# Where the paged decode's value pages are multiplied: pairs inside the seams behind the output projections and in cross attention, in place of dummy products

## The chip, the cores and the metric

The kernel runs on one core of a Trainium2 chip. The metric is the device time of one launch in microseconds, the median of several runs. TensorE (PE) multiplies and transposes, and loads its weights ahead (PEld); VectorE (DVE) and ScalarE (ACT) work elementwise and along rows; GpSimd (POOL) here does small power functions and issues the gathers of cache pages; SyncE (SP) issues the other loads and stores. The order of each engine's instructions is fixed when the program is recorded.

## What is computed

One layer of a hybrid decoder on two groups that share weights: a prompt of 1024 rows by 1024, and eight sample rows, each of which attends to 64 cached pages of 128 positions.

```python
q, k, v, logf, u, z = mixer_inputs(rmsnorm(xp, g_mix[l]), w_in[l], b_f[l], g_sgu_v[l])
xp = xp + merge_heads(fox_prompt(q, k, v, logf), sgu_prompt(u, z, w_s[l], b_s[l]),
                      g_att_out[l], g_sgu_out[l], w_o[l])
mk, mv = memory_kv(mem_prompt, g_mem[l], w_ck[l], w_cv[l])
xp = xp + cross_attend(rmsnorm(xp, g_cross[l]), mk, mv, w_cq[l], w_co[l])
f, conv_p = conv_ffn(rmsnorm(xp, g_ffn[l]), jnp.zeros((bp, CONV_W - 1, 2 * D_FF), xp.dtype),
                     w_up[l], conv_w[l], conv_b[l], w_down[l])
xp = xp + f
...
att = fox_sample(q, k, v, logf, cache_k[l], cache_v[l], cache_logf[l], page_table)
```

`fox_sample` is what the text calls the decode: scores of one query row against all cached keys of its sequence, a softmax with a forget gate, and the weighted sum of the cached values. In the kernel the cache of a sequence is read in sixteen steps, each of which gathers 128 pieces of four positions: one tile of 128 x 2048 numbers, which the text calls a page (128 K pages and 128 V pages in all, 1 MB each).

## The kernel before

**Stages.** The prompt goes in two halves of 512 rows (four row blocks of 128). After the input projection and attention each half hf runs through three stages: the output projection w_o with its residual ("mid"), cross attention with its own projections w_cq and w_co, and the convolutional FFN. Every large product is made of three (high and low halves of both operands: L272 to L274, L280 to L284, L1063 to L1065 and L1081 to L1083), so PE does most of the work.

**A seam.** Between an output projection and the next stage the rows must be normalized and transposed, which nothing of the next stage can precede. `out_proj` (L1023) does the left 512 columns for all row blocks, then the right 512 columns in groups: row block 0, row block 1, row blocks 2 and 3 together. After each group `residual` (L1011) adds the product to x on DVE (L1015) and squares it on ACT (L230, `ssq_into`). `factor` (L1028) makes 1/rms of a row block from that: ACT L1031, then POOL L1032 (a power). Behind w_co, `scaled` and `both` scale the rows: y0, y1 on ACT, y2 on ACT (L1044) and y3 on DVE (L1045), the last two in halves. Behind w_o the rows go on unscaled. `norm_T` (L1104) transposes two row blocks at a time on PE (L1124, t0 = 0, then t0 = 2), and `split` makes the high half on ACT (L238) and the low half on DVE (L239). `first` starts the next stage's product with what is there: `gemm3_late` (L276) first issues the products that need high halves (L280 and L281: one column half each), and then those with the low half (L284). The seams in the trace: mid0 at about 545 to 580 us, w_co to the first FFN at about 690 to 708, mid1 at 1170 to 1185, w_co to the second FFN at 1320 to 1336.

**Dummies.** For the late half of the seams behind w_co (`late`), `fill` (L1098) issues eight products (L1102, 128 x 256) of numbers that are at hand into a psum tile which the transposes then overwrite. Nothing reads them.

**The decode in the background.** `sample()` is a generator. The prompt's generator yields the time that it thinks its last piece takes, and the loop at the end of the program runs a decode step whenever enough has gathered (`PACE`, by stage), but none while `held[0]` is set. A K step gathers a K page with POOL (L1428), multiplies it by the query on DVE (L1444) and sums it (L1448). A V step gathers with POOL (L1489) and multiplies on PE (L1495) into one psum tile for a sequence. V steps come in pairs of pages: a pair is requested in one step of the decode and multiplied in the next. The trace shows a pair as sixteen L1495, the order as eight. K and V pages share one pool of four buffers (`NKV`), so a page's gather waits until the page four before it has been used. `held[0]` is set after the group of row blocks 2 and 3 and cleared when `norm_T` ends. `mix` runs two generators side by side; `gating(1)`, a piece of the second half's spatial gating, runs beside the first half's cross attention (ratio 0.05), and what is left of it then runs later.

**Order.** The tile framework records the instructions through a scheduler: `tc.high_priority()` raises a piece, and `tc.issue_after(x)` keeps an instruction behind x. The order on each engine is what comes out of that.

## Time and profile before

| | us |
|---|---|
| runs: 1789.9, 1795.0, 1800.49; median | 1795.0 |
| the profiled execution, its span | 1791.7 |
| PE busy in it | 1735.9 |
| DVE busy | 1399.9 |
| ACT busy | 733.5 |
| POOL busy | 488.3 |
| the 1024 products of V pages (L1495), busy | 127.1 |
| gathers of V pages on POOL (L1489, 128) | 160.8 |

The span holds the whole execution. A row of the timeline names the start, the duration, the engine, the line and operation, what is written from what, and how many such instructions follow one another; in brackets stands the idle time before it, and what ended it. PE's ends are modelled and rows overlap, so the time that an instruction occupies PE is read from the distance of two starts. Tiles: `u` is the pool of working rows and their split halves, `ba` and `bb` are two psum pools, `fac` holds 1/rms, `gp` the gains, `wh` and `wl` a weight's halves, `kv` a page, `dv` the sum of values, `s` the decode's scores.

### The profile page before, as it was taken

To read this page: it belongs to the slowest core of one execution; us is meant where nothing else is said; L and a number is where in the kernel's file an instruction comes from. 1 tells how busy PE (TensorE), PEld (TensorE's weight loads), DVE (VectorE), ACT (ScalarE), POOL (GpSimd) and SP (SyncE) were. 2 spreads that over 40 slices of the span, in tenths; PEclk is the share of its full clock that TensorE was granted. 3 is DMA by queue.
4 is the path that set the end of the run, shared out by engine and by line. 5 is a ranking of instruction groups with operands and counts; after the bars stand their busy time and mean duration, and the time that the engine had idled before them with its cause. 6 is when DMAs were issued, how large, how long until landed. Compare 5 with 4: busy or idle time off the path is not lost.

```text
span 1791.7 us, 25124 instructions
## 1 busy us (share of the span) xinstructions
PE 1735.9 (97%) x9653; PEld 1285.7 (72%) x9653; DVE 1399.9 (78%) x1733; ACT 733.5 (41%) x1374; POOL 488.3 (27%) x461
## 2 busy tenths in 40 slices
PE   8999999889999999999999999999999999999997
PEld 5787777655677666767777777766666778768875
DVE  4689658989788986989999999898885549855344
ACT  6332355566643635333333244335353233333232
POOL 1252234443222332333322223433322112102110
PEclk9999999999999999999999999999999999999999
DMA  8786798777697975779788788988879587568982
GB/s 291 297 304 226 294 334 319 259 264 244 254 403 279 363 299 224 282 285 345 290 301 313 291 317 311 376 306 346 320 280 350 214 306 249 191 260 297 359 310 80
DMA packets 157074, 521.06 MB, mean 291 GB/s; under 512 B 20874, under 2 KB 40842, under 8 KB 124186
## 3 DMA queue, kind: packets, MB, share of 16 engines
q0 software_dynamic: 57168, 341.14, 50.0%
q1 hardware_dynamic: 92874, 165.73, 26.5%
q10 hardware_dynamic: 6912, 12.59, 1.9%
q8 instruction: 76, 1.25, 0.3%
q14 instruction: 44, 0.36, 0.1%
HBM read 495.47 MB, written 23.93 MB: 290 GB/s over the span
## 4 chain that ended last, share of the span: by engine, by line
PE 53%; issue 9%; DMA 8%; DVE 6%; ACT 2%; POOL 2%; POOLq 0%; DVEq 0%; ACTq 0%; SPq 0%
DMA kv<-cache_v,io 6%; PE ba L272 6%; PE ba L274 6%; PE ba L273 6%; PE dv L1495 4%; PE bb L272 3%; PE bb L273 3%; PE bb L274 3%; PE ba L1063 1%; DVE s L1448 1%; PE ba L1064 1%; PE ba L1065 1%; PE dv L331 1%; DMA kv<-cache_k,io 1%; PE dv L1774 1%
## 5 line engine op out<-in xcount | busy, mean ns | idle before, releaser
L235 ACT ACTIVATE wh<-wr 128x1024 fp32r<-128x1024 f32 (+2 forms) x220 | 228.6, 1044 | 443.3 <-PE ba L273 142.3
L236 DVE TENSOR_TENSOR wl<-wr,wh 128x1024 fp32r<-128x1024 f32 (+2 forms) x220 | 262.7, 1200 | 165.1 <-PE ba L274 57.4
L1428 POOL DMA_INDIRECT kv<-cache_k,io x128 | 186.9, 1460 | 606.8 <-DVE s L1448 327.2
L1444 DVE TENSOR_TENSOR kv<-kv,d 128x1024 f32<-128x1024 f32 (+1 forms) x156 | 258.0, 1681 | 32.6 <-DMA kv<-cache_k,io 32.6
L1448 DVE TENSOR_REDUCE s<-kv 128x16 f32<-128x1024 f32 (+1 forms) x156 | 258.4, 1672 | 0.0
L1489 POOL DMA_INDIRECT kv<-cache_v,io x128 | 160.8, 1256 | 239.4 <-PE dv L1495 155.2
L272 PE MATMUL ba<-u,wh 128*128 128x512 f32 x528 | 209.3, 397 | 0.0
L274 PE MATMUL ba<-u,wl 128*128 128x512 f32 x528 | 209.0, 396 | 0.0
L273 PE MATMUL ba<-u,wh 128*128 128x512 f32 x528 | 208.5, 395 | 0.5 <-DVE u L239 0.5
L272 PE MATMUL ba<-wh,u 128*128 128x512 f32 (+1 forms) x495 | 186.1, 379 | 0.9 <-ACT u L235 0.9
L273 PE MATMUL ba<-wl,u 128*128 128x512 f32 (+1 forms) x495 | 185.1, 375 | 1.3 <-DVE wl L236 1.3
L274 PE MATMUL ba<-wh,u 128*128 128x512 f32 (+1 forms) x495 | 183.4, 375 | 0.0
L1495 PE MATMUL dv<-kv,s 128*32 128x512 f32 x1024 | 127.1, 598 | 1.6 <-DMA kv<-cache_v,io 1.6
L274 PEld LDWEIGHTS ba<-u,wl 128*128 128x128 f32 x528 | 99.2, 188 | 29.0 <-issue 6.5
L272 PEld LDWEIGHTS ba<-u,wh 128*128 128x128 f32 x528 | 99.3, 188 | 26.4 <-issue 4.8
L273 PEld LDWEIGHTS ba<-u,wh 128*128 128x128 f32 x528 | 99.2, 188 | 25.2 <-issue 2.3
L272 PEld LDWEIGHTS ba<-wh,u 128*128 128x128 f32 x495 | 93.0, 188 | 25.0 <-issue 6.5
L272 PE MATMUL bb<-u,wh 128*128 128x512 f32 x272 | 108.7, 400 | 0.0
L274 PE MATMUL bb<-u,wl 128*128 128x512 f32 x272 | 108.0, 398 | 0.0
L273 PE MATMUL bb<-u,wh 128*128 128x512 f32 x272 | 107.9, 397 | 0.0
L273 PEld LDWEIGHTS ba<-wl,u 128*128 128x128 f32 x495 | 93.0, 188 | 20.1 <-DVE wl L236 1.9
L274 PEld LDWEIGHTS ba<-wh,u 128*128 128x128 f32 x495 | 92.9, 188 | 19.5 <-issue 1.6
(454 smaller groups left out, 3310.6 us busy)
## 6 DMA issues: line engine op xcount, KB each, us to landing
wr<-w_up SPq DMA_DIRECT2D x88, 512.0 KB
kv<-w_up POOLq DMA_DIRECT2D x22, 1024.0 KB
wr<-w_down SPq DMA_DIRECT2D x40, 512.0 KB
kv<-w_down POOLq DMA_DIRECT2D x11, 1024.0 KB
wr<-w_in SPq DMA_DIRECT2D x16, 512.0 KB
wr<-w_o SPq DMA_DIRECT2D x16, 512.0 KB
wr<-w_cq SPq DMA_DIRECT2D x16, 512.0 KB
wr<-w_co SPq DMA_DIRECT2D x16, 512.0 KB
```

The costliest lines, as they stand in the source:

```text
L235: nc.scalar.activation(h, src, AF.Copy)
L236: nc.vector.tensor_tensor(l, src, h.bitcast(F32), op=ALU.subtract)
L272: mmul(out, sh, mh, start=(i == 0), stop=False)
L273: mmul(out, sh, ml, start=False, stop=False)
L274: mmul(out, sl, mh, start=False, stop=(i == n - 1))
L331: mmul(ps[32 * j : 32 * j + 32, :w], xT[:, k, :] if nk == 8 else xT[:, k * 8 : k * 8 + 32], raw[:, q, j * w : (j + 1) * w], start=(k == 0) ...
L1063: mmul(pss[i], mh[k][:, tb], wh, start=(k == korder[0]), stop=False)
L1428: nc.gpsimd.indirect_dma_start(kv, None, a["cache_k"], off(kidx[:, b, ch : ch + 1]))
L1444: nc.vector.tensor_tensor(kvv[:, i : i + m, :], kvv[:, i : i + m, :], qb.unsqueeze(1).broadcast_to((P, m, 512)), op=ALU.mult)
L1448: nc.vector.tensor_reduce(s[:, ch * 4 + i : ch * 4 + i + m, :].rearrange("p k h -> p (k h)"), kvv[:, i : i + m, :].rearrange("p k (h d) -> ...
L1489: nc.gpsimd.indirect_dma_start(kv, None, a["cache_v"], off(kidx[:, b, ch : ch + 1]))
L1495: mmul(dv[32 * j : 32 * j + 32, :], s[:, ch * 4 : ch * 4 + 4, :].rearrange("p k h -> p (k h)"), kvv[:, j, :], start=(ch == 1), stop=(ch == ...
```

## The change

1. `out_proj` sets `held[0]` before the products of row blocks 2 and 3 at the right columns instead of behind them, and there calls `ask_ahead`, which requests V pages for up to two pairs.
2. `norm_T` calls `give_now(2)`, which multiplies up to two pairs that have been requested: in front of the late transposes in place of `fill` (`fill` remains where no pair is at hand), and in every `norm_T` in front of `first` of the second half.
3. Cross attention multiplies up to one pair at the start of each `gather`; between `keys(2)` and the output projection (`lazy[0]`) pairs are multiplied nowhere else.
4. The decode keeps its pairs in a queue (`pend`), counts those requested (`asked`) and those whose softmax exists (`able`), and ends a sequence (`vend`) when its last pair is done and none is pending. In "mid" stages it requests a pair only while more than two can be requested, or more than two are due.
5. In `both` y2's scaling is issued behind the newest square (row block 3's).
6. `gating(1)` runs beside cross attention at ratio 0.08 instead of 0.05.

```diff
+            squared[:] = [newest(ENG.Activation)]
...
-        def both(r2, r3):
+        def both(r2, r3, end):
 
             y2, y3 = U([P, D]), U([P, D])
             for c in (slice(0, 512), slice(512, D)):
-                nc.scalar.activation(y2[:, c], xt[2][:, c], AF.Copy, scale=r2)
+                with tc.issue_after(end):
+                    nc.scalar.activation(y2[:, c], xt[2][:, c], AF.Copy, scale=r2)
...
             for group in ((0,), (1,), (2, 3)):
+                if len(group) == 2:
+                    held[0] = True
+                    if burst:
+                        burst[0]()
...
-                held[0] = len(group) == 2
                 yield 5.2
...
-                ys.append(partial(both, factor(2), factor(3)))
+                end = squared[0]
+                ys.append(partial(both, factor(2), factor(3), end))
...
-                if late and kk == 0:
+                if late and kk == 0 and not (burst and burst[1](2)):
                     fill(tr, hs)
...
+            if t0 and burst:
+                burst[1](2)
             first(hs, ls, c)
...
         def gather(h):
+            if burst:
+                burst[1](1)
...
+        lazy[0] = True
         keys(2)
...
             gather(h)
             yield 4
+        lazy[0] = False
...
+        pend, masked = [], []
+        asked, able = [0], [0]
+        def ask():
+
+            vb, i = divmod(asked[0], 8)
+            if i == 0:
+                dv[vb] = DV()
+            two = [(2 * i, KV()), (2 * i + 1, KV())]
+            if i % 2:
+                two.reverse()
+            pend.append((vb, i, [vstep(vb, c, st[vb], dv[vb], kv) for c, kv in two]))
+            asked[0] += 1
+
+        def give():
+
+            vb, i, mms = pend.pop(0)
+            mms[1]()
+            mms[0](newest(ENG.PE))
+            if i == 7:
+                vm[vb] = vmask(vb, dv[vb])
+                masked.append(vb)
+
+        def ask_ahead():
+            while len(pend) < 2 and asked[0] < able[0] and (not pend or asked[0] % 8):
+                ask()
+
+        def give_now(n):
+            k = 0
+            while pend and k < n:
+                with tc.issue_after(newest(ENG.PE)):
+                    give()
+                k += 1
+            return k
+
+        burst[:] = [ask_ahead, give_now]
...
+            if masked and not pend:
+                vend(masked[0], vm[masked.pop()])
...
+                able[0] = b * 8
...
+            while pend and not lazy[0]:
+                give()
+            n = (g - 16 - VLAG) // 2
+            due = min(n + (g - 16 - VLAG) % 2, 64) - asked[0]
+            spare = able[0] - asked[0] if phase[0][:3] == "mid" and g < 128 else 9
+            if not pend and due > 0 and (spare > 2 or due > 2):
+                ask()
...
-                ys = yield from mix(cross(xt, sq), gating(1), 0.05)
+                ys = yield from mix(cross(xt, sq), gating(1), 0.08)
```

The order on the engines at three places. In the changed program L1124 is L1131, L1495 is L1509, L1044 is L1047 and L1031 is L1033; L230, L238, L280, L281 and L284 keep their numbers.

PE in the seam from w_co to the first FFN, before, from the first late transpose on (`u_6373` is y2; `bb_6340` and the like are psum tiles for transposes, `ba_6304` is the FFN's first product):

```order
L1124 MATMUL bb_6405<-cp,u_6373 128x128
L280 MATMUL ba_6304<-u_6338,wh_6301 128x256
L281 MATMUL ba_6304<-u_6338,wl_6300 128x256
L284 MATMUL ba_6304<-u_6306,wh_6301 128x256 x2
L284 MATMUL ba_6304<-u_6317,wh_6301 128x256 x2
L284 MATMUL ba_6304<-u_6328,wh_6301 128x256 x2
L284 MATMUL ba_6304<-u_6339,wh_6301 128x256 x2
L1102 MATMUL ba_6379<-u_6305 128x256
L1124 MATMUL ba_6396<-cp,u_6373 128x128
L1124 MATMUL ba_6414<-cp,u_6373 128x128
L1102 MATMUL ba_6379<-u_6305 128x256
L1102 MATMUL ba_6379<-u_6316 128x256 x2
```

and now (`u_6360` is y2, `u_6361` y3; `kv` and `dv` belong to the decode):

```order
L1131 MATMUL ba_6409<-cp,u_6360 128x128
L280 MATMUL ba_6291<-u_6325,wh_6288 128x256
L281 MATMUL ba_6291<-u_6325,wl_6287 128x256
L284 MATMUL ba_6291<-u_6293,wh_6288 128x256 x2
L284 MATMUL ba_6291<-u_6304,wh_6288 128x256 x2
L284 MATMUL ba_6291<-u_6315,wh_6288 128x256 x2
L284 MATMUL ba_6291<-u_6326,wh_6288 128x256 x2
L1509 MATMUL dv_5415<-kv_6177,s_2862 32x512 x4
L1509 MATMUL dv_5415<-kv_6178,s_2862 32x512 x4
L1509 MATMUL dv_5415<-kv_6215,s_2862 32x512
L1131 MATMUL ba_6366<-cp,u_6361 128x128
L1131 MATMUL ba_6391<-cp,u_6361 128x128
```

In place of the dummies stand a whole pair and one row of a second; four transposes of y2 (the first row is the last of them) stand ahead of the last L280, one before. Behind the twelve transposes, of which two are shown, follow the other seven rows of the second pair.

PE in the seam from w_co to the second FFN, before (`u_11104` is y2, `u_11105` y3):

```order
L284 MATMUL ba_11035<-u_11037,wh_11032 128x256 x2
L284 MATMUL ba_11035<-u_11048,wh_11032 128x256 x2
L284 MATMUL ba_11035<-u_11059,wh_11032 128x256 x2
L284 MATMUL ba_11035<-u_11070,wh_11032 128x256
L1124 MATMUL ba_11127<-cp,u_11104 128x128
L284 MATMUL ba_11035<-u_11070,wh_11032 128x256
L1102 MATMUL bb_11110<-u_11036 128x256 x2
L1102 MATMUL bb_11110<-u_11047 128x256 x2
L1102 MATMUL bb_11110<-u_11058 128x256 x2
L1102 MATMUL bb_11110<-u_11069 128x256 x2
L1124 MATMUL bb_11110<-cp,u_11104 128x128
```

and now (`u_11081` is y2, `u_11082` y3):

```order
L1131 MATMUL bb_11132<-cp,u_11082 128x128
L280 MATMUL ba_11012<-u_11046,wh_11009 128x256
L281 MATMUL ba_11012<-u_11046,wl_11008 128x256
L284 MATMUL ba_11012<-u_11014,wh_11009 128x256 x2
L284 MATMUL ba_11012<-u_11025,wh_11009 128x256 x2
L1131 MATMUL ba_11123<-cp,u_11081 128x128
L1131 MATMUL ba_11123<-cp,u_11082 128x128
L1131 MATMUL ba_11123<-cp,u_11081 128x128
L1131 MATMUL ba_11123<-cp,u_11082 128x128
L284 MATMUL ba_11012<-u_11036,wh_11009 128x256 x2
L284 MATMUL ba_11012<-u_11047,wh_11009 128x256 x2
L1509 MATMUL dv_10153<-kv_10932,s_8605 32x512 x4
```

The first row here is the last of twelve transposes of y2 and y3 in a row; before, all late transposes but one stood behind the products. Two pairs stand behind the last L284, one row of which is shown.

ACT in the seam from w_co to the first FFN, before (`sqx` holds the sums of squares, `u_4762` is row block 2, `u_4764` row block 3):

```order
L230 ACTIVATE junk_6274,sqx_5897<-u_4762 128x512
L238 ACTIVATE u_6338<-bb_6340,gp 128x256
L1031 ACTIVATE fac_1257_6279<-sqx_5897,part_5898 128x1
L1044 ACTIVATE u_6373<-u_4762,fac_1257_6279 128x512 x2
L230 ACTIVATE junk_6277,sqx_5897<-u_4764 128x512
L238 ACTIVATE u_6338<-bb_6340,gp 128x256
L1031 ACTIVATE fac_1258_6282<-sqx_5897,part_5898 128x1
L230 ACTIVATE junk_6285,ssu_5123<-u_5806 128x512
```

and now:

```order
L230 ACTIVATE junk_6274,sqx_5930<-u_4762 128x512
L238 ACTIVATE u_6325<-bb_6327,gp 128x256
L1033 ACTIVATE fac_1259_6279<-sqx_5930,part_5931 128x1
L230 ACTIVATE junk_6277,sqx_5930<-u_4764 128x512
L1047 ACTIVATE u_6360<-u_4762,fac_1259_6279 128x512 x2
L1033 ACTIVATE fac_1260_6282<-sqx_5930,part_5931 128x1
L238 ACTIVATE u_6325<-bb_6327,gp 128x256
L238 ACTIVATE u_6303<-ba_6391,gp 128x256
```

Row block 3's square has moved ahead of y2's scaling, and the squares of the gating (`ssu`) have left this place.

More of the change, by code (lines that the diff above doesn't have):

```diff
@@ L1006, in build @@
     held = [False]
+    squared = []
     def squares():
@@ L1366, in build @@
     last = {}
+    burst, lazy = [], [False]
     bgs, acc, phase = [], [0.0], ["p1", None]
@@ L1524, in decode @@
         st, A, dt_, pm, dg, dv, vm = ([None] * 8 for _ in range(7))
-        pend = []
+        pend, masked = [], []
[27 more added lines that the diff above has]
+        burst[:] = [ask_ahead, give_now]
         st[0] = prep(0)
@@ L1528, in decode @@
             b, ch = divmod(g, 16)
-            if ch == VLAG + 1 and 2 <= b < 10:
-                vend(b - 2, vm[b - 2])
+            if masked and not pend:
+                vend(masked[0], vm[masked.pop()])
             if ch == 0 and 1 <= b < 9:
@@ L1545, in decode @@
                     pm[b] = soft_max(b, st[b], dt_[b])
-            if pend:
-                pend.pop()()
-                pend.pop()(newest(ENG.PE))
-                if vch == 15:
-                    vm[vb] = vmask(vb, dv[vb])
-            vb, vch = divmod(g - 16 - VLAG, 16)
-            if 0 <= vb < 8 and vch % 2:
-                if vch == 1:
-                    dv[vb] = DV()
-                two = [(vch - 1, KV()), (vch, KV())]
-                if vch % 4 == 3:
-                    two.reverse()
-                pend += [vstep(vb, c, st[vb], dv[vb], kv) for c, kv in two]
+            while pend and not lazy[0]:
[5 more added lines that the diff above has]
+                ask()
             yield left
+        if masked:
+            vend(masked[0], vm[masked[0]])
+        burst.clear()
     rows8 = []
```

## The prediction

> **What bounds the kernel now.** I read the head of the page first, then busy time in stretches of 100 us, then finer stretches, then the timelines of the seams.
>
> ```profile
> span 1791.7 us, 25124 instructions
> PE 1735.9 (97%) x9653; PEld 1285.7 (72%) x9653; DVE 1399.9 (78%) x1733; ACT 733.5 (41%) x1374; POOL 488.3 (27%) x461
> ...
> 600.00:700.00 100.00, 94.63 (x459) 65.49 (x456) 83.60 (x100) 49.28 (x111) 32.63 (x27) 1.00 0.79 308
> ...
> 800.00:900.00 100.00, 100.00 (x478) 73.11 (x477) 97.00 (x89) 31.89 (x51) 31.80 (x24) 1.00 0.85 323
> 1300.00:1400.00 100.00, 97.22 (x534) 66.30 (x533) 65.54 (x94) 43.65 (x85) 26.09 (x27) 1.00 0.83 315
> ```
>
> Columns after the length: PE, PEld, DVE, ACT and POOL busy, granted clock, DMA share, GB/s. PE is the bound: a microsecond is won only where PE idles or multiplies something nobody needs. In 800 to 900 DVE, at 97.00, is nearly a second bound. The change touches the two seams where w_co ends and the FFN begins; I call them B (near 700 us) and D (near 1330 us). In finer stretches:
>
> ```profile
> 680.00:685.00 5.00, 5.00 (x30) 2.74 (x30) 5.00 (x5) 3.16 (x3) 0.99 (x2) 1.00 0.00 0
> ...
> 695.00:700.00 5.00, 2.15 (x12) 1.76 (x13) 1.99 (x6) 4.29 (x12) 1.11 (x2) 0.96 1.00 419
> 700.00:705.00 5.00, 5.00 (x31) 4.75 (x29) 3.05 (x9) 1.63 (x7) 1.01 (x1) 0.70 0.68 270
> ```
>
> In 680 to 685 the DMA queues have nothing to do; in 695 to 700 they are full. There PE first stands still for 2.85 of 5 us; then it is busy, but at a granted clock of 0.70, which costs 5 x 0.30 = 1.5 us. PE's timeline of B:
>
> ```profile
> 694.00 0.39 PE L280 MATMUL ba<-u,wh 128*128 128x256 f32 x1 [0.32 <-ACT u L238]
> ...
> 695.51 0.38 PE L280 MATMUL ba<-u,wh 128*128 128x256 f32 x1 [0.57 <-DVE u L239]
> ...
> 697.71 0.33 PE L1124 MATMUL bb<-cp,u 128*128 128x128 f32 x1 [1.70 <-ACT u L1044]
> 698.68 0.39 PE L280 MATMUL ba<-u,wh 128*128 128x256 f32 x1 [0.64 <-ACT u L238]
> ...
> 699.02 1.46 PE L284 MATMUL ba<-u,wh 128*128 128x256 f32 x8
> 700.27 0.41 PE L1102 MATMUL ba<-u 128*128 128x256 f32 x1
> ...
> 700.77 1.84 PE L1102 MATMUL ba<-u 128*128 128x256 f32 x7
> 702.41 1.21 PE L1124 MATMUL ba<-cp,u 128*128 128x128 f32 x7
> ...
> 704.07 0.38 PE L280 MATMUL ba<-u,wh 128*128 128x256 f32 x1
> ```
>
> Brackets hold the idle time and what ended it: 0.32 + 0.57 + 1.70 + 0.64 = 3.23 us of waiting, and 0.41 + 1.84 = 2.25 us of dummies (L1102). The longest wait is for y2, scaled on ACT. The chain behind it, on ACT, POOL and DVE:
>
> ```profile
> 695.35 0.29 ACT L1031 ACTIVATE fac<-sqx,part 128x1 f32<-128x1 f32 x1
> 696.32 1.33 ACT L1044 ACTIVATE u<-u,fac 128x512 f32<-128x512 f32 x2 [0.68 <-POOL fac L1032]
> 697.56 0.61 ACT L230 ACTIVATE junk<-u 128x512 bf16<-128x512 f32 x1
> ...
> 698.53 0.28 ACT L1031 ACTIVATE fac<-sqx,part 128x1 f32<-128x1 f32 x1
> ...
> 694.05 0.68 DVE L1015 TENSOR_TENSOR u<-ba,u 128x512 f32<-128x512 f32 x1
> ...
> 699.47 0.88 DVE L1045 TENSOR_SCALAR u<-u,fac 128x512 f32<-128x512 f32 x2 [0.33 <-POOL fac L1032]
> ```
>
> Row block 3 is complete on DVE by 694.73, but its Square runs on ACT only at 697.56, behind y2. ACT itself waits 0.68 us for POOL just before y2. D, with the pair that stands before it:
>
> ```profile
> 1322.23 1.92 PE L1495 MATMUL dv<-kv,s 128*32 128x512 f32 x16
> 1324.08 0.50 PE L1083 MATMUL ba<-wh,u 128*128 128x512 f32 x1
> ...
> 1325.11 0.27 PE L1468 MATMUL ms<-cp,pm 128*8 128x128 f32 x1
> 1326.43 0.39 PE L280 MATMUL ba<-u,wh 128*128 128x256 f32 x1 [1.05 <-DVE u L239]
> ...
> 1329.34 0.51 PE L284 MATMUL ba<-u,wh 128*128 128x256 f32 x2 [0.18 <-DVE u L239]
> 1330.61 0.33 PE L1124 MATMUL ba<-cp,u 128*128 128x128 f32 x1 [0.77 <-ACT u L1044]
> ...
> 1330.90 1.11 PE L1102 MATMUL bb<-u 128*128 128x256 f32 x8
> ...
> 1333.02 0.17 PE L1616 MATMUL ms<-cp,mT 8*8 8x8 f32 x1 [0.51 <-DVE s L1483]
> 1333.42 0.33 PE L1124 MATMUL bb<-cp,u 128*128 128x128 f32 x1 [0.23 <-DVE u L1045]
> ...
> 1335.13 0.36 PE L280 MATMUL ba<-u,wh 128*128 128x256 f32 x1
> ...
> 1326.32 0.96 ACT L238 ACTIVATE u<-ba,gp 128x256 fp32r<-128x256 f32 x2
> ```
>
> Here 2.74 us are waits and 1.11 us dummies. So B and D hold 3.23 + 2.25 + 2.74 + 1.11 = 9.33 us that useful work could fill, and the low clock another 1.5. The first two rows give the price of a pair: 1324.08 - 1322.23 = 1.85 us of PE. Its products are needed anyway: moving a pair gains only what it covers at its new place.
>
> **Seam B.** In the new order two pairs, 3.70 us, stand in it, and the dummies are gone: 9 of their 16 rows behind the eight L284, then twelve late transposes, then 7 rows, then the first late L280. Before y2, ACT now does row block 3's Square, which fits mostly into its 0.68 us of waiting; y2 keeps its time to about 0.1 us. fac3 loses the Square from its path, so y3, ready at 699.47 + 0.88 = 700.35 before, comes about 0.6 us earlier. Four transposes of y2 instead of one stand ahead of the last L280, all waiting for the same y2, so the 1.70 us stays. I count from the end of the eight L284, 700.27: 9/16 of 3.70 is 2.08; thirteen transposes lie between 702.41 and 704.07, 0.128 each, twelve 1.53; 7/16 of 3.70 is 1.62. The late L280 then comes at 700.27 + 2.08 + 1.53 + 1.62 = 705.5, against 704.07: the seam is 1.4 us longer and holds 3.70 us that stood elsewhere, a gain of 2.3. y3 is there before the transposes reach it, so the pairs hide it; without them it would be waited for. New on POOL are the pairs' V pages ahead of fac0 and fac1, the last of them behind a buffer that a K page's reduce on DVE sets free. That reduce stands on DVE ahead of the residual that fac1 needs anyway, so fac1 loses one issue of about a microsecond at most, and y1, which follows it, is wanted only after w_co's last 48 products. The pages are asked for before those products, 48 x 0.26 = 12 us ahead (four of them lie between 1324.08 and 1325.11 in D's rows below), where the DMA queues stood empty. Bounds: everything filled, 3.23 + 2.25 = 5.5 of gain; nothing, if a page lands late. For the clock I take half of 1.5, 0.7 of gain, bounds 0 and 1.5.
>
> **Seam D.** Two pairs stand behind the last L284, but twelve late transposes, y3's among them, now stand ahead of the last L280 and of all L284, and on ACT seven splits (L238) stand ahead of y2. From the end of w_co the path is, by the rows of B: Square 0.61 and fac 0.29, each twice, and y2 1.33, with seven splits at the 0.48 of D's ACT row: 1.80 + 1.33 + 3.36 = 6.5 us, against 1330.61 - 1325.11 = 5.5 before. Then PE does sixteen transposes, 2.05, L280 and eight L284, 1.3 by the 1.11 of eight products as wide, and the pairs last: 6.5 + 3.4 + 3.7 = 13.6 us, of which 3.7 are pairs; 9.9 without them, against 1335.13 - 1325.11 = 10.0. The end of w_co comes earlier by the pair that no longer stands there, which is not counted twice. I take 0, bounds 2 of gain (DVE's K work is gone sooner) and 2 of loss (a split waits longer).
>
> **Cross attention and w_o.**
>
> ```profile
> 618.35 3.72 PE L1188 MATMUL ba<-t,u 128*128 128x256 f32 x16 [1.23 <-ACT t L1175]
> ...
> 626.71 1.92 PE L1495 MATMUL dv<-kv,s 128*32 128x512 f32 x16 [0.33 <-DMA kv<-cache_v,io]
> ...
> 1259.55 1.13 PE L1216 MATMUL ba<-u,t 128*128 128x512 f32 x2 [1.03 <-ACT u L1209]
> ...
> 1179.52 0.39 PE L280 MATMUL bb<-u,wh 128*128 128x256 f32 x1 [1.70 <-ACT u L238]
> ```
>
> A pair now stands before each gather (L1216) and would cover the third row's 1.03; the first row's wait is in front of L1188, where none is put. I take 1.0 of gain, bounds 2.3 (both waits) and 2 of loss (a late page like the second row's, 0.33, several times). Between w_o and the cross projections the 1.70 us of the last row stays: the pair stood behind it and does so still, so 0, give or take 1.
>
> **Elsewhere.** Pages and pairs are the same in number. The sample's end comes 4 us earlier in PE's order, and PE still has the prompt's last products after it, so the tail gains nothing. Gating at 0.08 moves its products from the FFN into cross attention, the same work: 0, give or take 1. K pages cost DVE:
>
> ```profile
> L1444 DVE TENSOR_TENSOR kv<-kv,d 128x1024 f32<-128x1024 f32 (+1 forms) x156 | 258.0, 1681 | 32.6 <-DMA kv<-cache_k,io 32.6
> L1448 DVE TENSOR_REDUCE s<-kv 128x16 f32<-128x1024 f32 (+1 forms) x156 | 258.4, 1672 | 0.0
> ```
>
> (258.0 + 258.4) / 128 pages = 4.0 us each. By the order, 62 instead of 63 are done when the first FFN begins: 4.0 us more for DVE there, against 100 - 97.00 = 3.0 spare in one of its three stretches of 100; 0, up to 1 of loss.
>
> **Sum.** -2.3 - 0.7 + 0 - 1.0 = -4.0 us: 1791.7 - 4.0 = 1787.7 for a profiled execution. The median of the runs, 1795.0, lies 3.3 above the profiled span, which is the whole of that execution; on the runs' scale 1791.0.
>
> **Rivals.** Half a percent of 1795.0 is 9 us, about what a measurement of this kernel can tell from no change.
>
> (a) The seams close wholly. For it: waits and dummies together are as long as four pairs, 9.33 against 7.4 us. Against it: in both seams y2's wait stands in PE's order ahead of the pairs, and PE takes them in order. It gives -9.33 - 1.5 - 2.3 = -13.1: 1778.6, 1782 on the runs' scale.
>
> (b) The clock falls without the dummies, and pairs run at half rate. For it: 0.70 in 700 to 705 although no wait in B passed 1.70 us. Against it: 0.96 in the stretch before. Pairs in B would cost 3.7 more, -4.0 + 0.7 + 3.7 = +0.4: 1792.1, 1795. The Trainium skill, "TensorE: Matmul & The Clock Gate", Part 1, states a gate that is either full or half, set by how busy the array was in a free-running window of about 3.4 us; by that rule the dummies bought nothing in B, as the 0.70 among them agrees, and pairs behind the same stall would start slow too.
>
> (c) Slower: K pages pushed into the first FFN. While a seam is held no page is started, and V pages fill the four kv buffers; four K pages then stand in a row on POOL behind fac3, and the count is one behind. If DVE has to take these five at once, 5 x 4.0 = 20.0 us meet 3.0 of spare, wl (L236) comes late and PE waits 17.0; with 4.0 won, +13.0: 1804.7, 1808. It decides once more than 4.0 + 3.0 = 7.0 us of DVE work, two pages, must be done at once. For it: DVE at 97.00. Against it: the count of one page.
>
> (d) The pairs only change places: the seams grow by what they take in, 1791.7, 1795.
>
> **Chances.** Forecast 0.46, (a) 0.18, (b) 0.07, (c) 0.20, (d) 0.09. The forecast's own bounds, its terms not all at their ends together, are 1784 to 1797; the range, out past (a) and to the near side of (c), is 1778 to 1806. Faster by over 0.5% (under 1786): (a) and a third of the forecast, 0.33. Slower (over 1804): (c) and 0.03 of the others' upper ends, 0.23. Within: 0.44.
>
> **What would show it.** B right: no L1102, two pairs between the last L284 and the late L280, Square of row block 3 before y2, the wait for y2 still there at 1.5 to 2 us, and 4 us or more of new cover. D right: a wait of 3 to 4 us in front of the twelve transposes. Clock: 700 to 705 above 0.85. (a): waits under 1 us in both. (c): PE under 99 us in 700:800 or 800:900, waiting for wl. It is wrong if pairs wait for pages (DMA named in front of the pair's line), or if a seam's residual comes late on DVE.

## The result, and the profile after

The changed kernel takes 1805.95 us (median of 20 runs, 1797.62 to 1812.39), the kernel before 1797.34 (20 runs, 1789.9 to 1805.28). The ratio is 1.0048, 95% interval 1.0035 to 1.0061: 8.6 us slower, about half a percent. The forecast was 4 us faster. The profiled executions differ by 1801.9 - 1791.7 = 10.2 us.

The head of the page after, and the groups of the V pages (product and gather):

```profile
span 1801.9 us, 25107 instructions
PE 1734.2 (96%) x9637; PEld 1284.1 (71%) x9637; DVE 1397.0 (78%) x1731; ACT 735.3 (41%) x1376; POOL 510.5 (28%) x461
...
L1503 POOL DMA_INDIRECT kv<-cache_v,io x128 | 177.4, 1386 | 305.3 <-PE dv L1509 134.0
...
L1509 PE MATMUL dv<-kv,s 128*32 128x512 f32 x1024 | 125.7, 603 | 5.1 <-DMA kv<-cache_v,io 4.9
```

PE does no more work than before (1734.2 against 1735.9 us; sixteen dummies are gone); it waits longer, 1801.9 - 1734.2 = 67.7 us against 1791.7 - 1735.9 = 55.8. To see where, I cut the span at the same events in both kernels: the first score product of cross attention (L1188, now L1197), the start of w_co's right columns, the last transpose of the seam, the start of w_o's right columns. Busy time between them, for the first cross attention, the seam behind its w_co, the stretch from the first FFN to the second half's w_o, the second cross attention and the seam behind it, before:

```profile
577.50:662.40 84.90, 82.76 (x397) 57.05 (x396) 74.60 (x88) 40.78 (x100) 27.18 (x22) 1.00 0.87 338
662.40:704.00 41.60, 38.37 (x202) 28.82 (x202) 30.69 (x43) 20.39 (x45) 13.00 (x12) 0.96 0.69 278
704.00:1143.50 439.50, 437.20 (x2083) 326.06 (x2082) 411.56 (x394) 158.51 (x248) 131.84 (x94) 1.00 0.81 303
1211.90:1296.70 84.80, 81.95 (x389) 53.71 (x388) 73.97 (x78) 40.49 (x96) 30.08 (x24) 1.00 0.87 328
1296.70:1334.70 38.00, 35.23 (x197) 26.13 (x196) 31.95 (x43) 20.53 (x45) 12.22 (x12) 1.00 0.88 350
```

and after:

```profile
581.20:667.40 86.20, 80.30 (x365) 54.13 (x364) 76.15 (x95) 38.82 (x98) 28.88 (x20) 0.96 0.85 308
667.40:703.60 36.20, 34.55 (x189) 25.48 (x187) 25.11 (x33) 18.90 (x42) 12.90 (x11) 1.00 0.71 251
703.60:1149.10 445.50, 439.36 (x2081) 327.06 (x2079) 411.10 (x392) 157.68 (x247) 150.30 (x94) 1.00 0.82 304
1221.20:1306.50 85.30, 78.24 (x364) 52.70 (x363) 76.17 (x80) 38.26 (x93) 27.04 (x23) 0.98 0.83 313
1306.50:1341.10 34.60, 32.36 (x166) 25.72 (x165) 30.75 (x43) 20.18 (x45) 8.22 (x9) 0.95 0.81 303
```

Length less PE's busy time is PE's waiting: in the two cross attentions 2.14 + 2.85 = 5.0 us before, 5.90 + 7.06 = 13.0 after, and the granted clock fell from 1.00 to 0.96 and 0.98; in the long stretch behind the first seam 2.3 before, 6.1 after. These two places hold the loss: 8.0 and 3.8 of the 11.9 us of new waiting. Over the whole span the mean clock of these two executions is the same, 0.993: from 300 to 400 us the kernel before ran at 0.93 and the changed one at 0.98. Over the 20 runs of the changed kernel the mean clock is 0.991, over the 23 runs of the kernel before that stand beside cross_plain, an experiment below, 0.995. The seam to the first FFN itself went as forecast. Before, PE was busy for 2.15 of 5 us in the first of these fine stretches, and the clock was 0.70 in the second:

```profile
695.00:700.00 5.00, 3.35 (x22) 2.11 (x24) 2.55 (x6) 3.14 (x9) 1.08 (x2) 1.00 0.33 105
700.00:705.00 5.00, 5.00 (x41) 2.18 (x36) 0.95 (x3) 1.46 (x5) 1.93 (x2) 1.00 0.46 143
```

PE's timeline of it, then ACT's and DVE's rows for row block 3's square (L230), y2 (L1047), fac3 (L1033) and y3 (L1048):

```profile
697.07 0.44 PE L1131 MATMUL ba<-cp,u 128*128 128x128 f32 x2 [1.05 <-ACT u L1047]
...
698.57 1.11 PE L284 MATMUL ba<-u,wh 128*128 128x256 f32 x8
699.61 2.76 PE L1509 MATMUL dv<-kv,s 128*32 128x512 f32 x18
702.30 0.44 PE L1131 MATMUL ba<-cp,u 128*128 128x128 f32 x2
...
703.76 1.92 PE L1509 MATMUL dv<-kv,s 128*32 128x512 f32 x14
705.61 0.39 PE L280 MATMUL ba<-u,wh 128*128 128x256 f32 x1
...
695.55 0.62 ACT L230 ACTIVATE junk<-u 128x512 bf16<-128x512 f32 x1
...
696.30 1.33 ACT L1047 ACTIVATE u<-u,fac 128x512 f32<-128x512 f32 x2
697.54 0.28 ACT L1033 ACTIVATE fac<-sqx,part 128x1 f32<-128x1 f32 x1
...
698.61 0.88 DVE L1048 TENSOR_SCALAR u<-u,fac 128x512 f32<-128x512 f32 x2
```

Two pairs stand in the seam, the square runs where ACT used to wait for POOL, y2 keeps its time, and no transpose waits for y3. The second FFN's seam:

```profile
1331.22 0.49 PE L1131 MATMUL ba<-cp,u 128*128 128x128 f32 x3
...
1333.64 0.38 PE L280 MATMUL ba<-u,wh 128*128 128x256 f32 x1 [0.94 <-ACT u L238]
...
1335.70 0.58 PE L280 MATMUL ba<-u,wh 128*128 128x256 f32 x1 [1.16 <-ACT u L238]
...
1336.30 0.41 PE L280 MATMUL ba<-u,wh 128*128 128x256 f32 x1
1336.51 0.41 PE L281 MATMUL ba<-u,wl 128*128 128x256 f32 x1
...
1339.96 0.36 PE L280 MATMUL ba<-u,wh 128*128 128x256 f32 x1
...
1341.11 0.70 PE L284 MATMUL ba<-u,wh 128*128 128x256 f32 x4
1341.74 2.78 PE L1509 MATMUL dv<-kv,s 128*32 128x512 f32 x24
```

0.94 + 1.16 = 2.1 us of waits, and 2.24 with the small ones, against 2.74 before, but for the early splits (L238), not for y2. Its products run slowly: L280 and L281 start 0.21 us apart at 1336.30, and the eight L284 of the other seam took 699.61 - 698.57 = 1.04, 0.13 each. That is the clock of 0.95 in the last row of the stages. In cross attention PE waits for ACT and for V pages:

```profile
601.18 1.16 PE L649 MATMUL bb<-u,u 128*128 128x128 f32 x8 [1.24 <-ACT u L1205]
...
613.03 0.33 PE L1217 MATMUL bb<-cp,u 128*128 128x128 f32 x1 [1.47 <-ACT u L1210]
616.27 3.78 PE L1197 MATMUL ba<-t,u 128*128 128x256 f32 x8 [1.61 <-ACT u L1205]
...
1244.55 3.72 PE L1197 MATMUL ba<-t,u 128*128 128x256 f32 x16 [1.84 <-ACT t L1184]
...
1254.47 1.92 PE L1509 MATMUL dv<-kv,s 128*32 128x512 f32 x16 [2.76 <-DMA kv<-cache_v,io]
...
1259.73 2.62 PE L1197 MATMUL ba<-t,u 128*128 128x256 f32 x7 [1.88 <-ACT t L1184]
```

What stands ahead of the second of these waits: a group of score products (L1197), K work on DVE (L1458, L1462), behind it the maximum of these scores (L1199) and the reciprocal of the softmax's sums (L1208), then ACT's scaling (L1210), for which PE waits. Last, POOL's gather of the page that the pair at 1254.47 waits for:

```profile
603.18 1.89 PE L1197 MATMUL ba<-t,u 128*128 128x256 f32 x8
...
608.00 2.34 DVE L1458 TENSOR_TENSOR kv<-kv,d 128x1024 f32<-128x1024 f32 x2
610.26 1.20 DVE L1462 TENSOR_REDUCE s<-kv 128x16 f32<-128x1024 f32 x1
611.39 0.67 DVE L1199 TENSOR_REDUCE cmx<-ba 128x2 f32<-128x512 f32 x1
611.99 0.15 DVE L1208 RECIPROCAL cr<-cl 128x4 f32<-128x4 f32 x1
...
611.59 0.60 ACT L1184 ACTIVATE t<-ba 128x512 f32<-128x512 f32 x1 [3.65 <-PE ba L1180]
...
612.48 1.69 ACT L1210 ACTIVATE u<-u,cr 128x256 f32<-128x256 f32 x4
...
1242.05 0.95 POOL L1503 DMA_INDIRECT kv<-cache_v,io  x1 [0.30 <-PE ba L1180]
```

In this wait DVE is not alone: ACT had stood for PE's transposes (L1180) until 611.59, and the reciprocal was done at 612.14, before ACT reached its scaling. What DVE does there shows in the maximum: the scores were ready at 605.1, and it began at 611.39. Each cross attention has eight such groups of scores. Counting in both traces DVE's K work between the end of a group's products and its maximum, I find 14.8 us before and 50.5 after, for the two stages together, although the first stage holds as many K pages as before (10.5).

The gather was issued 1254.47 - 1242.05 = 12.4 us before its pair could start. Why POOL comes late shows in what its V gathers wait for, over the whole span. Before:

```profile
  PE dv L1495: 155.2, 41
  DVE s L1448: 39.1, 13
```

After:

```profile
  PE dv L1509: 134.0, 34
  DVE s L1462: 122.2, 22
```

A V gather waits for a buffer, which either an earlier pair's products (first row; us, then times) or a K page's reduction (second row) sets free. The second kind went from 39.1 to 122.2 us: V pages are asked for while K pages still hold the buffers, and the next K page is queued on POOL behind that. POOL stands no longer in all: the same two waits of the K gathers fell from 327.2 + 127.5 to 284.6 + 111.1 us, so the four together are 649 us before and 652 after. What changed is the order in which the pages come, and when.

### The profile page after: what moved, and what is told of

Its sections match the earlier page's. It is cut to its first block, busy times and chain, and to the rows that moved or that the text cites. A ratio compares the mean times of both kernels' runs of the same rounds, so it can differ in the third digit from the quotient of the medians.

```text
span 1801.9 us, 25107 instructions
## 1 busy us (share of the span) xinstructions
PE 1734.2 (96%) x9637; PEld 1284.1 (71%) x9637; DVE 1397.0 (78%) x1731; ACT 735.3 (41%) x1376; POOL 510.5 (28%) x461
## 4 chain that ended last, share of the span: by engine, by line
PE 38%; issue 13%; DVE 13%; DMA 11%; POOL 3%; ACT 2%; POOLq 0%; DVEq 0%; SPq 0%; ACTq 0%
PE ba L274 4%; PE ba L272 4%; PE ba L273 3%; PE dv L1509 3%; DVE kv L1458 3%; DMA kv<-cache_v,io 3%; DMA kv<-cache_k,io 3%; DVE s L1462 2%; PE bb L272 2%; PE bb L274 2%; PE bb L273 2%; DMA kv<-w_up 2%; POOL kv L1503 2%; DVE wl L236 1%; PE ba L1068 1%
## 5 line engine op out<-in xcount | busy, mean ns | idle before, releaser
L1442 POOL DMA_INDIRECT kv<-cache_k,io x128 | 186.4, 1456 | 525.0 <-DVE s L1462 284.6
L1458 DVE TENSOR_TENSOR kv<-kv,d 128x1024 f32<-128x1024 f32 (+1 forms) x155 | 258.3, 1693 | 29.0 <-DMA kv<-cache_k,io 28.2
L1503 POOL DMA_INDIRECT kv<-cache_v,io x128 | 177.4, 1386 | 305.3 <-PE dv L1509 134.0
L1462 DVE TENSOR_REDUCE s<-kv 128x16 f32<-128x1024 f32 (+1 forms) x155 | 258.4, 1685 | 0.0
L273 PE MATMUL ba<-u,wh 128*128 128x512 f32 x536 | 212.1, 396 | 1.6 <-DVE u L239 1.6
L272 PE MATMUL ba<-u,wh 128*128 128x512 f32 x536 | 212.5, 397 | 0.0
L1509 PE MATMUL dv<-kv,s 128*32 128x512 f32 x1024 | 125.7, 603 | 5.1 <-DMA kv<-cache_v,io 4.9
L272 PE MATMUL bb<-u,wh 128*128 128x512 f32 x264 | 104.6, 396 | 0.0
L273 PE MATMUL bb<-u,wh 128*128 128x512 f32 x264 | 104.5, 396 | 0.0
```

Of the source, the lines that this page charges most:

```text
L272: mmul(out, sh, mh, start=(i == 0), stop=False)
L273: mmul(out, sh, ml, start=False, stop=False)
L1442: nc.gpsimd.indirect_dma_start(kv, None, a["cache_k"], off(kidx[:, b, ch : ch + 1]))
L1458: nc.vector.tensor_tensor(kvv[:, i : i + m, :], kvv[:, i : i + m, :], qb.unsqueeze(1).broadcast_to((P, m, 512)), op=ALU.mult)
L1462: nc.vector.tensor_reduce(s[:, ch * 4 + i : ch * 4 + i + m, :].rearrange("p k h -> p (k h)"), kvv[:, i : i + m, :].rearrange("p k (h d) -> ...
L1503: nc.gpsimd.indirect_dma_start(kv, None, a["cache_v"], off(kidx[:, b, ch : ch + 1]))
```

## The experiments

Each was compared with the kernel before on the same chip. The ratio has its 95% interval. "Cross" and "FFN" are PE's idle times in the profiled execution, in the two cross attentions and in the long stretch behind the first seam, cut as above; "V waits" is the second kind of the last fences.

| kernel | ratio | cross, us | FFN, us | V waits on DVE, us |
|---|---|---|---|---|
| before | 1 | 5.0 | 2.3 | 39 |
| changed | 1.0048 (1.0035 to 1.0061) | 13.0 | 6.1 | 122 |
| cross_plain | 1.0066 (1.0045 to 1.0087) | 13.9 | 6.6 | 129 |
| ratio05 | 1.0054 (1.0033 to 1.0075) | 11.1 | 8.4 | 95 |
| seams_alone | 1.0045 (1.0028 to 1.0061) | 12.0 | 5.5 | 102 |
| late_hold | 1.0089 (1.0067 to 1.0110) | 9.9 | 7.2 | 115 |
| co_only | 1.0058 (1.0036 to 1.0081) | 10.5 | 6.6 | 72 |
| o_only | 1.0047 (1.0030 to 1.0064) | 12.7 | 1.7 | 91 |
| no_give_o | 1.0053 (1.0034 to 1.0072) | 12.3 | 5.3 | 127 |
| ask_only | 1.0072 (1.0058 to 1.0086) | 12.8 | 4.2 | 120 |
| seams_undone | 1.0009 (0.9996 to 1.0022) | 7.5 | 2.5 | 61 |
| hold_alone | 1.0026 (1.0014 to 1.0039) | 7.0 | 4.1 | 50 |
| swap_only | 0.9993 (0.9979 to 1.0007) | 7.1 | 2.0 | 56 |
| square_first | 0.9985 (0.9969 to 1.0000) | 5.2 | 1.8 | 44 |
| one_ahead | 0.9982 (0.9969 to 0.9996) | 7.5 | 3.3 | 67 |
| one_ahead_seams (one_ahead, repeated) | 1.0006 (0.9997 to 1.0015) | 6.5 | 2.8 | 66 |
| co_one_plain | 0.9997 (0.9983 to 1.0012) | 7.8 | 3.2 | 66 |
| seams_one_ahead | 1.0033 (1.0018 to 1.0049) | 10.8 | 3.4 | 62 |

The rows from changed to ask_only request two pairs ahead of a seam, those from seams_undone on one or none. The V waits do not rank the losses: co_only has 72 us and is 0.58% slower, one_ahead has 67 and is not slower.

**Is it cross attention, the gating, or the seams?** The waits stood in cross attention, so my first theory blamed the change's edits there.

cross_plain:

```diff
-            if burst:
-                burst[1](1)
...
-        lazy[0] = True
...
-        lazy[0] = False
```

> The changed kernel with cross attention left as before: no pair at the gathers, and the decode's own loop multiplies pairs there (the lazy flag is never set). Seams, request ahead and the gating's ratio 0.08 stay. Theory C (the loss is in cross attention, where pairs held back for the gathers no longer cover the waits for the softmax and are waited for themselves): PE's waits in the two cross attentions fall from 5.9 and 7.1 us to 2 to 3 each, the half-rate clock inside them goes too, and the kernel stands 0 to 4 us under before. Theory S (the loss comes from the seams: the earlier hold and the pairs requested ahead push K pages and V pages onto the stages behind): still 5 us or more above before. Theory G (the gating at 0.08 loads ACT in the first cross attention): the first cross attention keeps 4 us or more of waits, the second falls, and the kernel stands about 3 us above before.

ratio05:

```diff
-                ys = yield from mix(cross(xt, sq), gating(1), 0.08)
+                ys = yield from mix(cross(xt, sq), gating(1), 0.05)
```

> The changed kernel with the gating at 0.05 as before. Theory G: the first cross attention's waits fall from 5.9 to about 2 us and the kernel comes down by 5 us or more. Theory C: at most 2 us come back, and the second cross attention, where no gating runs, keeps its 7 us of waits. Theory S: no change beyond 2 us.

seams_undone:

```diff
-                if len(group) == 2:
-                    held[0] = True
-                    if burst:
-                        burst[0]()
...
+                held[0] = len(group) == 2
...
-                if late and kk == 0 and not (burst and burst[1](2)):
+                if late and kk == 0:
...
-            if t0 and burst:
-                burst[1](2)
```

> The changed kernel with the seams as before: the hold is set behind the group of row blocks 2 and 3, no pair is requested ahead or multiplied in the seams, and the dummies are back; pairs only at the gathers in cross attention, gating at 0.08. Theory C: as slow as the changed kernel or up to 5 us slower, since the seams' gain of about 4 us goes and the loss in cross attention stays. Theory S: within 3 us of before.

seams_alone is cross_plain and ratio05 together.

> The changed kernel with cross attention and the gating's ratio as before: only the seams' part of the change is left. Theory C: 3 to 6 us under before (about 4 from the first FFN's seam with its clock, up to 1 from the second). Theory S: 5 us or more above before. Theory G: as theory C here.

Theory C fell: with cross attention as before its waits stayed (13.9 us), and with the seams undone, the edits in cross attention and the gating kept, the loss was gone (1.0009). G fell too: at 0.05 the first cross attention did not recover, and the kernel was 0.54% slower. S held: the seams' part alone costs 0.45%. What is late in cross attention is caused ahead of it.

**Which part of the seams?** hold_alone keeps the earlier hold, without the request and without pairs in the seams:

```diff
                     held[0] = True
-                    if burst:
-                        burst[0]()
...
-                if late and kk == 0 and not (burst and burst[1](2)):
+                if late and kk == 0:
...
-            if t0 and burst:
-                burst[1](2)
```

> The changed kernel with the earlier hold kept, but no pair requested ahead and none multiplied in the seams, dummies back. Theory H (the earlier hold costs: K pages that are not started in the seam come in a row behind it, DVE does their reductions in front of the softmax maxima of cross attention and of what the FFN needs, and PE waits): 5 us or more above before, with 5 us or more of PE waits in each cross attention. Theory P (the pairs requested ahead cost: V pages take the four buffers and POOL, K pages come late, and the pairs that cross attention could use are gone): within 2 us of the variant with undone seams, thus 0 to 4 above before.

late_hold keeps the request and the pairs:

```diff
-                    held[0] = True
...
+                held[0] = len(group) == 2
```

> The changed kernel with the hold set behind the group of row blocks 2 and 3, as before, but pairs requested ahead of that group and multiplied in the seams. Theory H: within 3 us of before, since K pages go on as before, and the first FFN's seam keeps part of its gain. Theory P: 5 us or more above before.

co_only and o_only make the seams' edits depend on `ys is not None` (behind w_co) or `ys is None` (behind w_o); o_only has its dummies back behind w_co.

> The changed kernel with its seam edits behind w_co alone; behind w_o the hold is late, nothing is requested ahead and nothing multiplied in the seam. If the loss arises behind w_o, where cross attention follows (both theories can say so): PE waits in the cross attentions fall to 4 us or less each, and the kernel stands 0 to 4 us under before. If it arises behind w_co, in the first FFN (rival (c) of the prediction): still 4 us or more above before, with the waits between 850 us and the second w_o at 3 us or more.

> The counterpart: seam edits behind w_o alone, dummies and late hold behind w_co. If the loss arises behind w_o: 5 us or more above before, cross attentions with 5 us or more of waits each. If behind w_co: within 2 us of the variant with undone seams.

H fell with late_hold, which it had within 3 us of before and which is 0.89% slower. For hold_alone both theories missed the time: it is 0.26% slower than before, by the ratio 4.7 us, where H had 5 or more and P 0 to 4, while its waits in cross attention, 4.1 and 2.9 us, speak against H. seams_undone stands at 0.09%, so the hold by itself costs some 0.2%. With the request, the early hold softens the loss (1.0048 against 1.0089): without it PE waits longer in the seams themselves, 5.0 us in that to the first FFN against 1.7 in the changed kernel. The two places lose in different stretches: o_only waits 12.7 us in cross attention and 1.7 in the FFN, co_only 6.6 in the FFN. But co_only kept 10.5 us in cross attention, which I had not expected of it (seams_undone has 7.5 there), and each place alone costs about as much as both. Why the two do not add up is open.

**Requesting or multiplying?** no_give_o multiplies no pair in the seam behind w_o but requests them there:

```diff
-            if t0 and burst:
+            if t0 and late and burst:
                 burst[1](2)
```

> The changed kernel in which no pair is multiplied in the seam behind w_o; the earlier hold and the pairs requested ahead stay there, so these pairs are multiplied in cross attention instead. Theory L (lost cover: PE has no idle time behind w_o, so a pair multiplied there covers nothing, and is missing in cross attention, where it would have stood in a wait): PE's waits in the two cross attentions fall from 13.0 us to 8 or less, and the kernel comes down by 4 us or more from the changed one. Theory K (late K pages: hold and V pages in the buffers push K work on DVE into cross attention, in front of the softmax's maxima): the waits stay at 11 us or more, and the time within 2 us of the changed kernel.

one_ahead requests one pair instead of two:

```diff
-            while len(pend) < 2 and asked[0] < able[0] and (not pend or asked[0] % 8):
+            while len(pend) < 1 and asked[0] < able[0] and (not pend or asked[0] % 8):
```

> The changed kernel with one pair requested ahead of a seam instead of two, so V pages take two of the four buffers. Theory K: K work moves less, and about half of the loss of 8.6 us comes back, in cross attention and in the first FFN alike. Theory L: one pair fewer is taken out of each cross attention, so about 4 us come back in cross attention too, but the first FFN keeps its waits of 6 us.

swap_only is seams_undone, but a pair that happens to be at hand behind w_co takes the dummies' place:

```diff
-                if late and kk == 0:
+                if late and kk == 0 and not (burst and burst[1](2)):
```

> The changed kernel with only the swap left in the seams: where a pair happens to be at hand behind w_co it is multiplied in place of the dummies, else the dummies stay; hold late, nothing requested ahead, nothing multiplied behind w_o. Both theories: within 2 us of the variant with undone seams, possibly 1 to 2 us under it, since only the second FFN's seam finds a pair.

ask_only has hold and request as changed, and multiplies in no seam:

```diff
-                if late and kk == 0 and not (burst and burst[1](2)):
+                if late and kk == 0:
...
-            if t0 and burst:
-                burst[1](2)
```

> The changed kernel that requests two pairs ahead with the earlier hold but multiplies none in the seams; dummies back behind w_co. Theory K (the four V pages of two requested pairs fill the four buffers, so K pages wait until the pairs are multiplied, and DVE gets them late and in a row): as slow as the changed kernel or slower, 6 us or more above before. If it were multiplying at these places that costs: within 3 us of the variant with undone seams.

L fell: without multiplying behind w_o the waits stayed at 12.3 us. swap_only, at 0.9993, which finds a pair in the second FFN's seam alone, shows no harm from a pair in the dummies' place. ask_only is the clearest: no pair is multiplied in any seam, and it is 0.72% slower. It differs from hold_alone by the request alone, and 1.0072 against 1.0026 is its price: 0.46%, some 8 us. With one pair instead of two the whole loss was gone, not half, as K had said. V gathers in ask_only:

```profile
  PE dv L1507: 144.3, 31
  DVE s L1460: 120.2, 24
```

and in one_ahead:

```profile
  PE dv L1509: 172.7, 39
  DVE s L1462: 66.8, 13
```

**The buffers.** The count of K work in front of the maxima, taken in every trace, goes by what is requested behind w_o: 44 to 53 us in the eight kernels that request two pairs there, 19 to 28 with one pair, 11 to 22 with none. So the request moves K work in front of the softmax. Whether it does so by filling the pool is another question. Four V pages are as many as the pool has buffers. Five buffers fit only with fewer weight tiles, so there is a base of its own, the kernel before with the same numbers:

```diff
-NKV = 4
+NKV = 5
...
-WH = 5
+WH = 4
...
-WR = 4
+WR = 3
```

> The kernel before with five page buffers instead of four, and to make room four weight high halves in place of five and three raw weights in place of four. The base for the next run; slower than before by an unknown amount for its shallower weights.

> The changed kernel with the same five, four and three. Theory K: with a fifth buffer one K page goes on while two pairs are held, so at least half of the 8.6 us between the changed kernel and before is gone when it is set against the run with five buffers before: at most 4 us above it. If buffers have nothing to do with it: 7 us or more above it.

1858.32 us before and 1850.78 changed (1.0379, 1.0362 to 1.0396, and 1.0340, 1.0325 to 1.0354, of the kernel before with four): with five buffers the changed kernel is 7.5 us the faster. That meets the number that theory K gave, but the trace takes part of it back. With the shallower weights PE waits in the seams behind w_o, mostly for DVE (24.2 us in five_before, 12.0 in five_after, 2.2 before), and that is where the difference lies; the cross attentions still wait 15.4 us, 8.8 of them once for a load of the memory's keys, against 2.7 in five_before. The waits there for ACT did fall, from 10.2 to 5.5, and none is for a V page any more; but 40.1 us of K work still stand in front of the maxima, against 15.7 in five_before. So a fifth buffer takes away little of that, and the place that the V pages take in POOL's queue remains a rival to the full pool. This pair of runs does not settle it.

**What is left of the gain?** square_first is the kernel before with y2 behind row block 3's square and nothing else (point 5 of the change).

> The kernel before with one edit: y2's scaling is issued behind row block 3's square. The prediction's working for the first FFN's seam: fac3 and y3 come about 0.6 us earlier; since y3 was not waited for there, 0 to 1 us is won, too little to be told from none; the second FFN's seam, where y3 was waited for 0.23 us, may give as much.

0.9985, its interval reaching 1: 2.3 us by the medians, at the edge of what can be told. PE's waits in the two seams, where the edit works, did not fall (7.0 us against 6.0 before). one_ahead once more:

> The variant with one pair requested ahead once more, beside kernels of this call. If its gain is real it stands 1 to 5 us under before again, as in its first measurement (0.9982).

1.0006: the gain of the first measurement was not repeated. co_one_plain leaves cross attention, the gating and the seam behind w_o as before, and behind w_co requests and multiplies one pair; seams_one_ahead does so behind w_o too:

```diff
-                if len(group) == 2:
+                if len(group) == 2 and ys is not None:
                     held[0] = True
                     if burst:
                         burst[0]()
...
-            if t0 and burst:
+            if late and burst:
                 burst[1](2)
```

> The kernel before with three parts of the change: y2 behind row block 3's square, the queue of pairs, and behind w_co alone the earlier hold with one pair requested ahead and multiplied in place of the dummies. Cross attention, the seam behind w_o and the gating's ratio are as before. If requesting two pairs was the whole loss, and the prediction's gain in the first FFN's seam is real: 2 to 5 us under before. If the seam's gain is given back by the K page that is late behind it: within 2 us of before.

> The same with one pair requested ahead and multiplied behind w_o too. There PE waits for nothing in the first half, so a pair gains nothing: within 2 us of the run beside it.

co_one_plain is as fast as before (0.9997): its waits and dummies in the two FFN seams fall by about 5 us, and cross attention and FFN wait 2.8 + 0.9 us more. seams_one_ahead missed its expectation, 0.33% slower: of its 10.8 us in cross attention 5.9 are waits of a pair for its page. Beside seams_alone, which requests two pairs and is otherwise the same kernel (1.0045, 1.0028 to 1.0061), its 1.0033 (1.0018 to 1.0049) cannot be told apart: one pair instead of two removed the loss only where cross attention and the gating are as changed. No version beat the kernel before by more than a measurement can tell.

## Why the prediction was wrong, by its steps

- **Seam B, right in its order, partly by luck in its time.** Forecast: the late L280 1.4 us later, at 705.5 if the eight L284 end at 700.27; measured 705.61, with the L284 ended at 699.61. The clock went to 1.00 as well, a gain of 1.5 where 0.7 was taken, and the wait for y2 was 1.05 instead of an unchanged 1.70. Two errors cancel in the 705.61: the L284 ended 0.66 us earlier, and the pairs, priced at 2.08 + 1.62, took (702.30 - 699.61) + (705.61 - 703.76) = 2.69 + 1.85 us, 0.84 more. In the trace such products start four at a time, about 0.43 us apart, and a pair split after one row leaves groups that are not full.
- **Seam D, about right.** Forecast 13.6 us from the end of w_co to the end of the pairs, no gain. w_co's products end where the transposes begin, at 1331.22, and the two pairs, 3.7 us, begin at 1341.74, so 14.2. The long wait that I put in front of the twelve transposes was not there; the early splits were waited for, and the clock fell to 0.95, which cost 34.6 x 0.05 = 1.7 us.
- **Cross attention, the step that failed.** The prediction took "1.0 of gain, bounds 2.3 (both waits) and 2 of loss". Measured: 8.0 us more of waits, and some 5 us of lost clock (86.2 x 0.04 + 85.3 x 0.02). Late V pages, which the bound of loss had foreseen, are 2.8 us of the 13.0; the waits for ACT grew from 4.7 to 10.2. The prediction looked only at where the new pairs stand, and never asked what the two V requests ahead of the stage do to the K pages whose DVE work runs inside it: that work now stands in front of the softmax's maxima, 50.5 us of it instead of 14.8. The "so 0, give or take 1" for the seam behind w_o is the same omission: PE there is as busy as before, and what was requested there costs 60 us and more behind it.
- **"the count of one page".** The K pages done at the FFN's start were 62 instead of 63, and I priced the rest of the backlog by that count, at 0 to 1 us. That count came true (62.0 in the trace). A count at one point says nothing of when the pages arrive between two points.
- **Rival (c)** had the mechanism in part: "V pages fill the four kv buffers". Its place was wrong: I put all of it into the FFN, where DVE is fullest, and 4 us arose there; twice as much arose in cross attention, where DVE has room on average (74.60 of 84.90 us) but the softmax waits for it in between. Nor did PE wait in the FFN for wl, as (c) had it: 2.3 us are pairs waiting for pages (1.3 before) and 2.4 waits for other results of DVE (0.8 before). The measured time lies near the (c) end of the range, but not by (c)'s way.
- **Rival (b)**, pairs at half rate in B without the dummies: the clock there was 1.00. **Rivals (a) and (d)** did not come.

In sum the seams behind w_co gave 5.4 us (their waits fell from 3.23 + 2.74 to 1.65 + 2.24, and 3.36 of dummies went), less the 0.84 of the split pairs, where 2.3 were forecast. Their clock, for which 0.7 of gain was taken, came to about nothing: 1.5 won in B, 1.7 lost in D. Against that stand 8.0 + 3.8 us of new waits in cross attention and the FFN and some 5 us of clock in cross attention. That requesting two pairs ahead is the cause of the loss in this kernel is shown by ask_only against hold_alone and by one_ahead against the changed kernel. That requests behind w_o move K work in front of the maxima in cross attention is shown by the count in the traces; that this makes all of PE's new waits there is argued, for co_only waits 10.5 us with 14.5 us of such work. Not settled are whether that comes from the full pool or from POOL's order, what makes the FFN's share, and why one pair instead of two makes no difference that can be told once cross attention and the gating are as before.

## What to carry to other kernels

That its use comes late does not make an early request free. Here it took a place in the issuing engine's queue and a buffer from a shared pool, and the other stream's work moved in front of a chain that PE waits for, one stage later. When a change moves requests, follow the pool they draw from and ask what else waits for it, instead of pricing only the place where the data is used. An engine with room on average (here DVE, busy for 74.60 of 84.90 us) can still be the one that a short chain (maxima, sums, scaling) waits for, so ask where in the stage its work falls, and not only how much of it there is.

## What the hardware showed that was not expected

The granted clock fell without any long wait. Waits of 1.47 and 1.61 us, 3 us apart (613.03 and 616.27), came with a clock of 0.96 over the first cross attention, and 1.84, 2.76 and 1.88 us with 0.98 over the second, where before waits of up to 1.23 us left it at 1.00. The loss is not spread: the trace has the clock at 0.50 from 615.4 to 622.2 and from 1260.6 to 1263.9. The Trainium skill, "TensorE: Matmul & The Clock Gate", section "Why this matters for your kernels", advises no idle gaps over about 3 us. The rows differ: no single gap here reached that, and several shorter ones close together went with the lower clock; that they caused it was not tried.
